# GpSimd instead of VectorE for the differences of weight blocks in the last down projection of a hybrid transformer block

## The chip, the cores and the metric

The kernel runs on one core of a Trainium2 chip. The metric is the device time of one execution in microseconds (us). A core has a matrix engine (TensorE, PE in the profile), three engines for elementwise work (VectorE or DVE, ScalarE or ACT, GpSimd or POOL) and a queue for transfers (SyncE or SP). Each engine works through its own list of instructions in order; semaphores make one engine wait for another. Operands lie in SBUF, and TensorE adds up its products in PSUM.

## The reference

The block has a first feed-forward part, a mixer (differential attention beside a causal convolution) and a second feed-forward part, each scaled by gates that come from a conditioning vector. Sequence length is 256, width 2048, the hidden width of the feed-forward parts 5632, everything float32. The part that the change touches is the last matrix product:

```python
def swiglu(h, w_gu, w_down):
    gu = jnp.einsum('bsd,df->bsf', h, w_gu)
    g, u = jnp.split(gu, 2, axis=-1)
    return jnp.einsum('bsf,fd->bsd', jax.nn.silu(g) * u, w_down)
...
h = modulate(rms_norm(x, ffn2_norm[l]), sh2, sc2)
x = x + FFN_RESIDUAL_WEIGHT * g2[:, None, :] * swiglu(h, ffn2_w_gu[l], ffn2_w_down[l])
```

Here `w_down` is 5632 x 2048, and the product is 256 x 5632 by 5632 x 2048.

## The kernel before

**Split products.** A float32 product is made of three TensorE products of a reduced format. Each operand is split into a high part, which ScalarE casts (`whi`, lines 303 and 510), and a low part, which VectorE subtracts from the original and the high part (`wlo`, lines 305 and 511). The three matmuls of `mm3` (lines 327, 331, 332) are high by high, high by low and low by high; the second reads the weights' low part, and all three have 512 columns.

**The last down projection** is `down_strassen`. It runs in two passes (`np_` 0 and 1), one for each half of the 2048 output columns. A pass has 22 steps, c = 0 to 21. A step loads one tile of weights (`raw`, four blocks of 128x512, 1 MB) and has two blocks of the hidden width, two row tiles and two column blocks.

- A plain step splits its tile in two pairs of blocks (lines 303 and 305, 128x1024 each) and makes eight products, 24 matmuls.
- Steps c = 3, 5, 8, 10, 13, 15 and 17 make seven products instead of eight (Strassen-Winograd), 21 matmuls. They need differences of weight blocks. With b11, b12, b21, b22 for the four blocks, line 545 makes t1 = b12 - b11 and t3 = b22 - b21 in place in one instruction of 128x1024; line 547 makes t2 = b22 - t1 and line 548 t4 = b21 - t2, 128x512 each. The splits follow one another: b11 (128x512), b21 and b22, then t1 and t3, then t4 and t2 (128x1024 each). So line 545 can start once b11's low part is there, the split of t1 and t3 follows line 545, line 547 needs the low parts of b21 and b22, and the split of t4 and t2 follows line 548.
- These steps also need sums of the activations, `sums_of`: a sum of 128x512 (line 483), four of 128x128 (486 to 489), a cast on ScalarE (500) and a low part on VectorE (501). Pass 0 makes all seven sets and six of them are kept for pass 1.

**What sets the order.** A scheduler places the instructions on each engine's list when the program is built, by priorities and its own estimates. High and low parts of weights have four buffers each (`whp`, `wlp`), so a cast waits until TensorE is done with the part four earlier. A plain step takes two buffers of each kind, a seven step all four. Weight tiles have four buffers as well (`rawp`). In a pass, after the last seven step (c = 17), four plain steps follow; VectorE combines the products of the seven steps there (lines 570 to 585). In pass 1 the matmuls of the last two steps are held back and run output tile by output tile, each followed by its scaling, its addition to the residual and its store (lines 528, 529 and 533).

Of the kernel before, what the change touches and what calls it, by code (L numbers as in the profile page):

```python
# [80 lines left out]
def block_kernel(ctx: ExitStack, tc: tile.TileContext, x_in, pos_in, w_ada, small, w_gu1, w_dn1,  # L81
                 w_in, w_out, w_gu2, w_dn2, out):
    nc = tc.nc
# [14 lines left out]
    def nm(s):  # L98
        uid[0] += 1
        return f"{s}_{uid[0]}"  # L100
# [4 lines left out]
    def tmp(shape, dtype=F32):  # L105
        return tmpp.tile(shape, dtype, tag="tmp", name=nm("tmp"))
# [4 lines left out]
    def acc_tile(shape=(P, 512)):  # L111
        return accp.tile(list(shape), F32, tag="acc", name=nm("acc"))
# [350 lines left out]
    def down_strassen(w_dn, aT, a_act, gate_of, evac_last, share, pend, finish):  # L463
# [13 lines left out]
        def sums_of(c):  # L477

            if c in kept:
                return kept[c]  # L480
            a = aT[c]
            full = tmp([P, 2, S])
            nc.vector.tensor_add(out=full, in0=a[:, 0].bitcast(F32), in1=a[:, 1].bitcast(F32))
            a11, a21, a12, a22 = full[:, 0, :P], full[:, 0, P:], full[:, 1, :P], full[:, 1, P:]
            q = tmp([P, 4, P])
            nc.vector.tensor_add(out=q[:, 0], in0=a21, in1=a22)
            nc.vector.tensor_sub(out=q[:, 1], in0=q[:, 0], in1=a11)
            nc.vector.tensor_sub(out=q[:, 2], in0=a11, in1=a21)
            nc.vector.tensor_sub(out=q[:, 3], in0=a12, in1=q[:, 1])
            i = SEVEN.index(c)  # L490
            keep = i < KEPT
            if keep:
                if i < 2:
                    sp = in_c_bc[:, i]
                else:
                    sp = blk([P, 2, 4, P], F32R)
                hi, lo = sp[:, 0], sp[:, 1]
            else:
                hi, lo = tmp([P, 4, P], F32R), tmp([P, 4, P], F32R)
            nc.scalar.copy(out=hi, in_=q)  # L500
            nc.vector.tensor_sub(out=lo, in0=q, in1=hi.bitcast(F32))
            res = [(hi[:, i], lo[:, i]) for i in range(4)]
            if keep:
                kept[c] = res
            return res
# [11 lines left out]
        for np_ in range(2):  # L517
            seven = [None] * 4
            held = []

            def place(i, np_=np_):
                t, n = order[i][0], 2 * np_ + order[i][1]
                return t, n, x[n][:, t, :]

            def final(i, acc, place=place):
                t, n, xs = place(i)
                m = tmp([P, 512])
                nc.vector.tensor_mul(out=m, in0=acc, in1=gbc[n])
                nc.vector.tensor_add(out=xs, in0=xs, in1=m)

            def store(i, place=place):
                t, n, xs = place(i)
                nc.sync.dma_start(out=out[t * P:(t + 1) * P, n * 512:(n + 1) * 512], in_=xs)

            for c in range(NCH):
                share()
                first, last = c == 0, c == NCH - 1
                if c in SEVEN:
                    raw = rawp.tile([P, 4, 512], F32, tag="raw", name=nm("raw"))
                    nc.sync.dma_start(out=raw, in_=w_dn[np_, c].rearrange("p (k n) -> p k n", k=4))  # L540
                    s1, s2, s3, s4 = sums_of(c)
                    (b11,) = split(raw[:, 0:1, :], 1)
                    b21, b22 = split(raw[:, 2:4, :], 2)

                    nc.vector.tensor_sub(out=raw[:, 0:2, :], in0=raw[:, 1:4:2, :], in1=raw[:, 0:2, :])
                    t1, t3 = split(raw[:, 0:2, :], 2)
                    nc.vector.tensor_sub(out=raw[:, 3, :], in0=raw[:, 3, :], in1=raw[:, 0, :])
                    nc.vector.tensor_sub(out=raw[:, 2, :], in0=raw[:, 2, :], in1=raw[:, 3, :])
                    t4, t2 = split(raw[:, 2:4, :], 2)
                    go, end = c == SEVEN[0], c == SEVEN[-1]  # L550
                    if go:
                        if np_ == 0:
                            seven = [acc_tile(), acc_tile(), tp_tile(), tp_tile()]
                        else:
                            seven = [acc_tile() for _ in range(4)]
                    mm3(seven[0], a_act(2 * c, 0), b11, go, end)
                    mm3(plain[0], a_act(2 * c + 1, 0), b21, False, False)
                    mm3(plain[1], s4, b22, False, False)
                    mm3(seven[1], s1, t1, go, end)
                    mm3(seven[3], s3, t3, go, end)  # L560
                    mm3(seven[2], s2, t2, go, end)
                    mm3(plain[2], a_act(2 * c + 1, 1), t4, False, False)
                    tick()
                    if end:

                        p1, p5, p6, p7 = seven
                        u = [tmp([P, 512]) for _ in range(5)]
                        last_pair = np_ == 1
                        nc.scalar.copy(out=u[0], in_=p1)
                        nc.vector.tensor_add(out=u[4], in0=p6, in1=u[0])  # L570

                        def step_1(u=u, p5=p5):
                            nc.vector.tensor_add(out=u[1], in0=p5, in1=u[4])

                        def step_2(u=u, p7=p7):
                            nc.vector.tensor_add(out=u[2], in0=p7, in1=u[4])

                        def step_3(u=u, p5=p5):
                            nc.vector.tensor_add(out=u[3], in0=p5, in1=u[2])

                        def add(i, u=u):

                            t, n, xs = place(i)
                            nc.vector.tensor_mul(out=u[i], in0=u[i], in1=gbc[n])
                            nc.vector.tensor_add(out=xs, in0=xs, in1=u[i])

                        if last_pair:
                            todo += [lambda: (step_1(), add(0), add(1)), lambda: (step_2(), step_3(), add(2)),
                                     lambda: add(3)]
                        else:  # L590
                            todo += [step_1, step_2, step_3]
                    continue
                w = w_tile(w_dn[np_, c])
                if np_ == 1 and c >= NCH - 2:
                    held.append((c, w))
                    if todo:
                        todo.pop(0)()
                    continue
                for k in range(2):
                    for i, (t, n) in enumerate(order):  # L600
                        mm3(plain[i], a_act(2 * c + k, t), w(2 * k + n), first and k == 0, last and k == 1)
                tick()
                if first and np_ == 0:
                    while pend:
                        finish(*pend.pop(0))
                    gbc = gate_of()
                if todo:
                    todo.pop(0)()
            if np_ == 0:
                while todo:  # L610
                    todo.pop(0)()

                def done(i, acc, u, place=place):
                    t, n, xs = place(i)
                    nc.vector.tensor_add(out=u, in0=acc, in1=u)
                    nc.vector.tensor_mul(out=u, in0=u, in1=gbc[n])
                    nc.vector.tensor_add(out=xs, in0=xs, in1=u)
                    nc.sync.dma_start(out=out[t * P:(t + 1) * P, n * 512:(n + 1) * 512], in_=xs)

                todo += [lambda p=plain, u=u: (done(0, p[0], u[0]), done(1, p[1], u[1])),  # L620
                         lambda p=plain, u=u: (done(2, p[2], u[2]), done(3, p[3], u[3]))]
                plain = [acc_tile(), acc_tile(), tp_tile(), tp_tile()]
                continue
            assert not todo
            for i, (t, n) in enumerate(order):
                with tc.issue_after(last_mm[0].ins) if i else nullcontext():
                    for c, w in held:
                        for k in range(2):
                            last_mm[0] = mm3(plain[i], a_act(2 * c + k, t), w(2 * k + n), False,
                                             c == NCH - 1 and k == 1)  # L630
                if i < 3:
                    final(i, plain[i])
                    store(i)
                else:
                    evac_last(2 + n, plain[i], t, gbc[2 + n])
# [820 lines left out]
```

## Time and profile before

| What | Value |
|---|---|
| Time, median of 3 runs | 1838.04 us (1837.12 to 1838.94) |
| The profiled execution: span from first to last instruction | 1835.9 us |
| TensorE, VectorE, ScalarE, GpSimd busy, whole span | 99%, 83%, 52%, 2% |
| Last down projection | about 1598 us to the end |
| Line 545, 14 instructions | 1.22 us each |
| Lines 547 and 548, 14 instructions each | 0.69 us each |

The profiled execution has no time of its own beside its span; the runs' median is 2.1 us more than that span. The page says for each engine how long it was busy. Its timeline gives an instruction's start, its duration, its engine, its line in the kernel, what it writes and reads, and in brackets how long the engine idled before it and what ended that. Instructions of one engine overlap by some hundredths of a microsecond, so the distance from one start to the next is the price of an instruction in an engine that is busy without a gap. A matmul shows 0.39 us, and one starts every 0.227 us.

### The profile page before, as it was taken

To read this page: it belongs to the slowest core of one execution; us is meant where nothing else is said; L and a number is where in the kernel's file an instruction comes from. 1 tells how busy PE (TensorE), PEld (TensorE's weight loads), DVE (VectorE), ACT (ScalarE), POOL (GpSimd) and SP (SyncE) were. 2 spreads that over 40 slices of the span, in tenths; PEclk is the share of its full clock that TensorE was granted. 3 is DMA by queue.
4 is the path that set the end of the run, shared out by engine and by line. 5 is a ranking of instruction groups with operands and counts; after the bars stand their busy time and mean duration, and the time that the engine had idled before them with its cause. 6 is when DMAs were issued, how large, how long until landed. Compare 5 with 4: busy or idle time off the path is not lost.

```text
span 1835.9 us, 22042 instructions
## 1 busy us (share of the span) xinstructions
PE 1812.0 (99%) x8205; PEld 1493.1 (81%) x8205; DVE 1521.8 (83%) x2018; ACT 960.7 (52%) x1477; POOL 28.3 (2%) x29
## 2 busy tenths in 40 slices
PE   7999999999999999999999999999999999999998
PEld 5788888888888887888888788888888888888887
DVE  7889869999888787898999768878877755699877
ACT  6554344444444343566798646664444444455453
POOL 0000000000000000000110000000000000000000
PEclk9999999999999999999999999999999999999999
DMA  9988978889899888765544467899777755555552
GB/s 375 352 307 300 352 272 301 343 306 340 336 322 357 353 343 329 289 256 187 181 159 161 161 229 294 315 335 339 263 273 284 285 197 188 184 206 208 205 210 111
DMA packets 72731, 495.93 MB, mean 270 GB/s; under 512 B 8192, under 2 KB 8624, under 8 KB 15152
## 3 DMA queue, kind: packets, MB, share of 16 engines
q1 hardware_dynamic: 72624, 494.53, 72.2%
q8 instruction: 64, 1.05, 0.2%
q14 instruction: 43, 0.35, 0.1%
HBM read 492.37 MB, written 2.12 MB: 269 GB/s over the span
## 4 chain that ended last, share of the span: by engine, by line
PE 90%; DVE 5%; ACT 2%; issue 1%; DMA 1%; POOL 0%; SPq 0%; POOLq 0%; DVEq 0%; ACTq 0%
PE acc L331 28%; PE acc L332 28%; PE acc L327 28%; DVE wlo L305 2%; PE tp L836 1%; PE tp L332 1%; PE tp L331 1%; PE tp L327 1%; DMA blk<-in_w_gu_dram 1%; PE acc L1123 1%; DVE blk L1015 1%; ACT whi L303 0%; PE tp L392 0%; DMA blk<-in_w_ada_dram 0%; DVE wlo L511 0%
## 5 line engine op out<-in xcount | busy, mean ns | idle before, releaser
L303 ACT CAST whi<-raw 128x1024 fp32r<-128x1024 f32 (+1 forms) x581 | 599.8, 1045 | 610.8 <-PE acc L332 450.3
L331 PE MATMUL acc<-wlo,blk 128*128 128x512 f32 x2340 | 913.5, 390 | 5.8 <-DVE wlo L305 5.8
L327 PE MATMUL acc<-whi,blk 128*128 128x512 f32 x2343 | 913.3, 393 | 1.7 <-ACT blk L401 1.3
L332 PE MATMUL acc<-whi,blk 128*128 128x512 f32 x2340 | 912.5, 390 | 0.1
L305 DVE TENSOR_TENSOR wlo<-raw,whi 128x1024 fp32r<-128x1024 f32 (+1 forms) x581 | 692.6, 1210 | 210.3 <-ACT whi L303 208.8
L331 PEld LDWEIGHTS acc<-wlo,blk 128*128 128x128 f32 x2340 | 439.6, 188 | 99.4 <-DVE wlo L305 10.3
L327 PEld LDWEIGHTS acc<-whi,blk 128*128 128x128 f32 x2343 | 440.0, 188 | 92.8 <-ACT blk L401 1.7
L332 PEld LDWEIGHTS acc<-whi,blk 128*128 128x128 f32 x2340 | 439.3, 188 | 92.4 <-DVE blk L403 0.7
L191 DVE CUSTOM_DVE_ANT_0 raw<-raw,c_bc 128x2048 f32<-128x2048 f32 x142 | 324.1, 2284 | 9.0 <-DMA raw<-in_w_ada_dram 8.8
L510 ACT CAST whi<-raw 128x1024 fp32r<-128x1024 f32 (+1 forms) x56 | 53.0, 946 | 70.2 <-PE tp L332 31.9
L511 DVE TENSOR_TENSOR wlo<-raw,whi 128x1024 fp32r<-128x1024 f32 (+1 forms) x56 | 60.9, 1088 | 19.0 <-ACT whi L510 18.7
L664 ACT COPY blk<-acc 128x512 f32<-128x512 f32 x72 | 41.9, 589 | 60.6 <-PE acc L332 57.9
L1015 DVE SCALAR_TENSOR_TENSOR blk<-blk,cst,blk 128x245 f32<-128x245 f32 (+21 forms) x176 | 70.5, 456 | 0.6 <-ACT blk L1013 0.5
L828 DVE TENSOR_TENSOR blk<-acc,blk 128x512 f32<-128x512 f32 x88 | 56.8, 682 | 0.2
L327 PE MATMUL acc<-blk,blk 128*128 128x512 f32 x104 | 41.3, 400 | 1.0 <-ACT blk L319 1.0
L332 PE MATMUL acc<-blk,blk 128*128 128x512 f32 x100 | 39.0, 392 | 0.0
L331 PE MATMUL acc<-blk,blk 128*128 128x512 f32 x100 | 39.0, 390 | 0.0
L830 DVE TENSOR_TENSOR blk<-blk 128x256 f32<-128x256 f32 x88 | 33.3, 417 | 0.7 <-ACT blk L829 0.7
L829 ACT ACTIVATE blk<-blk 128x256 f32<-128x256 f32 x88 | 32.2, 411 | 2.1 <-DVE blk L828 2.1
L349 DVE TENSOR_TENSOR blk<-tp,blk 128x512 fp32r<-128x512 f32 x44 | 29.9, 684 | 1.6 <-ACT blk L348 1.6
L305 DVE TENSOR_TENSOR blk<-raw,blk 128x1024 fp32r<-128x1024 f32 x24 | 28.8, 1218 | 0.8 <-ACT blk L303 0.8
L450 ACT ACTIVATE tmp<-tp,ada,scales 128x128 f32<-128x128 f32 x36 | 14.8, 459 | 28.0 <-DVE scales L233 15.5
(223 smaller groups left out, 1023.5 us busy)
## 6 DMA issues: line engine op xcount, KB each, us to landing
raw<-in_w_gu_dram SPq DMA_DIRECT2D x161, 1024.0 KB, 5.3
raw<-in_w_ada_dram SPq DMA_DIRECT2D x142, 1024.0 KB, 6.3
raw<-in_w_dn_dram SPq DMA_DIRECT2D x88, 1024.0 KB, 5.2
raw<-in_w_in_dram SPq DMA_DIRECT2D x40, 1024.0 KB, 4.8
raw<-in_w_out_dram SPq DMA_DIRECT2D x16, 1024.0 KB, 4.8
raw<-in_w_gu_dram SPq DMA_DIRECT2D x8, 768.0 KB, 6.0
blk<-in_w_gu_dram SPq DMA_DIRECT2D x10, 512.0 KB, 14.5
blk<-gate_line SPq DMA_DIRECT2D x6, 512.0 KB, 4.9
```

The source lines that it names most:

```text
L191: nc.vector.tensor_tensor_reduce(out=raw, in0=raw, in1=c_bc, scale=1.0, scalar=0.0, op0=ALU.mult, op1=ALU.add, accum_out=ada_cols[g][:, j ...
L303: nc.scalar.copy(out=hi[:, :m, :], in_=rw)
L305: nc.vector.tensor_sub(out=lo[:, :m, :], in0=rw, in1=hi[:, :m, :].bitcast(F32))
L327: nc.tensor.matmul(acc, ah, wh, start=start, stop=False)
L331: nc.tensor.matmul(acc, ah, wl, start=False, stop=False)
L332: return nc.tensor.matmul(acc, al, wh, start=False, stop=stop)
L510: nc.scalar.copy(out=hi[:, :n, :], in_=src)
L511: nc.vector.tensor_sub(out=lo[:, :n, :], in0=src, in1=hi[:, :n, :].bitcast(F32))
L664: last_part[0] = nc.scalar.copy(out=parts[c][:, t, :], in_=accs[t])
L828: nc.vector.tensor_add(out=p[:, t, :], in0=accs[t], in1=p[:, t, :])
L830: nc.vector.tensor_mul(out=p[:, t, 256:], in0=p[:, t, :256], in1=p[:, t, 256:])
L1015: nc.vector.scalar_tensor_tensor(out=y[:, d:], in0=u, scalar=w, in1=y[:, d:], op0=ALU.mult, op1=ALU.add)
```

## The change

In the steps with seven products the three subtractions of weight blocks are issued to GpSimd. Their operands, their sizes and what depends on them stay. All 14 such steps of the two passes are concerned, 42 instructions.

```diff
@@ -542,10 +542,10 @@
                     (b11,) = split(raw[:, 0:1, :], 1)
                     b21, b22 = split(raw[:, 2:4, :], 2)
 
-                    nc.vector.tensor_sub(out=raw[:, 0:2, :], in0=raw[:, 1:4:2, :], in1=raw[:, 0:2, :])
+                    nc.gpsimd.tensor_sub(out=raw[:, 0:2, :], in0=raw[:, 1:4:2, :], in1=raw[:, 0:2, :])
                     t1, t3 = split(raw[:, 0:2, :], 2)
-                    nc.vector.tensor_sub(out=raw[:, 3, :], in0=raw[:, 3, :], in1=raw[:, 0, :])
-                    nc.vector.tensor_sub(out=raw[:, 2, :], in0=raw[:, 2, :], in1=raw[:, 3, :])
+                    nc.gpsimd.tensor_sub(out=raw[:, 3, :], in0=raw[:, 3, :], in1=raw[:, 0, :])
+                    nc.gpsimd.tensor_sub(out=raw[:, 2, :], in0=raw[:, 2, :], in1=raw[:, 3, :])
                     t4, t2 = split(raw[:, 2:4, :], 2)
                     go, end = c == SEVEN[0], c == SEVEN[-1]
                     if go:
```

On VectorE the order changes in pass 0, since the scheduler places anew. This is step c = 5 (`raw_13078`); `in_c_bc` and `tmp` are the sums of activations, of this step and of the next seven steps.

```order
 L511 TENSOR_TENSOR wlo_13090<-raw_13078,whi_13089 128x512
-L489 TENSOR_TENSOR tmp_13082<-tmp_13080,tmp_13082 128x128
+L483 TENSOR_TENSOR tmp_13199<-blk_11373 128x512
 L511 TENSOR_TENSOR wlo_13094<-raw_13078,whi_13093 128x1024
 L501 TENSOR_TENSOR in_c_bc<-tmp_13082,in_c_bc 128x512
-L545 TENSOR_TENSOR raw_13078<-raw_13078 128x1024
-L483 TENSOR_TENSOR tmp_13199<-blk_11373 128x512
-L547 TENSOR_TENSOR raw_13078<-raw_13078 128x512
-L511 TENSOR_TENSOR wlo_13099<-raw_13078,whi_13098 128x1024
-L548 TENSOR_TENSOR raw_13078<-raw_13078 128x512
 L486 TENSOR_TENSOR tmp_13201<-tmp_13199 128x128
 L488 TENSOR_TENSOR tmp_13201<-tmp_13199 128x128
```

The three subtractions are gone, the sums for c = 8 move ahead of them, and the low part of t1 and t3 (`wlo_13099`) comes behind more of the sums. By the low parts of step c = 9 (`wlo_13253` and `wlo_13257`) the seventh set of sums is through:

```order
 L511 TENSOR_TENSOR wlo_13225<-raw_13197,whi_13224 128x1024
 L305 TENSOR_TENSOR wlo_13253<-raw_13249,whi_13251 128x1024
+L501 TENSOR_TENSOR tmp_13585<-tmp_13579,tmp_13584 128x512
 L305 TENSOR_TENSOR wlo_13257<-raw_13249,whi_13255 128x1024
 L511 TENSOR_TENSOR wlo_13296<-raw_13283,whi_13295 128x512
-L487 TENSOR_TENSOR tmp_13407<-tmp_13407,tmp_13405 128x128
-L545 TENSOR_TENSOR raw_13283<-raw_13283 128x1024
```

The sets for c = 13, 15 and 17 were made behind this place before. In pass 1 VectorE's order loses the three instructions and is otherwise the same. GpSimd's list had ended before the projection; now it has three subtractions for each step. These are the steps c = 5 and c = 8 of pass 0, with what each instruction waits for (DMAHW is a load, Pool is GpSimd itself):

```order
L545 TENSOR_TENSOR raw_13078<-raw_13078 128x1024 [waits DMAHW1_49,DMAHW5_49,DMAHW0_49,DVE_49]
L547 TENSOR_TENSOR raw_13078<-raw_13078 128x512 [waits DVE_49,Pool_49]
L548 TENSOR_TENSOR raw_13078<-raw_13078 128x512 [waits Pool_49]
L545 TENSOR_TENSOR raw_13197<-raw_13197 128x1024 [waits DMAHW3_49,DMAHW4_49,DMAHW2_49,DMAHW6_49,DMAHW0_49,DVE_49]
L547 TENSOR_TENSOR raw_13197<-raw_13197 128x512 [waits DVE_49,Pool_49]
L548 TENSOR_TENSOR raw_13197<-raw_13197 128x512 [waits Pool_49]
```

The first and the second subtraction wait for VectorE, and the second and the third for the one before. The order of transfers is unchanged; TensorE's changes in a few rows at c = 3 and c = 5 of pass 0.

## The prediction

> **What bounds the kernel now.** I read the page first, then the busy times of two stretches of the last down projection, then the timelines of VectorE and TensorE inside them, and last every place where GpSimd has worked beside VectorE.
>
> ```profile
> span 1835.9 us, 22042 instructions
> PE 1812.0 (99%) x8205; PEld 1493.1 (81%) x8205; DVE 1521.8 (83%) x2018; ACT 960.7 (52%) x1477; POOL 28.3 (2%) x29
> ```
>
> The profiled execution spans 1835.9 us. The median of the three runs is 1838.04, which is 2.1 us more; I add that at the end. TensorE is busy for 99% of the span, and GpSimd is nearly empty.
>
> ```profile
> core 0: us, PE busy (x) PEld busy (x) DVE busy (x) ACT busy (x) POOL busy (x), PEclk, DMA share, GB/s
> 1607.45:1647.03 39.58, 39.30 (x174) 31.65 (x173) 38.28 (x57) 21.99 (x26) 0.00 (x0) 1.00 0.51 192
> 1785.43:1822.50 37.07, 36.28 (x159) 29.39 (x157) 34.42 (x39) 19.10 (x20) 0.00 (x0) 1.00 0.38 142
> ...
> PE acc L331 <- DVE wlo L305: 0.8, 2, 0.7
> PE acc L327 <- ACT whi L303: 0.2, 1, 0.2
> ```
>
> These rows are two stretches and all that TensorE itself is seen to wait for from 1600 us to the end. The first stretch runs from the first VectorE instruction of step c=3 (pass 0) to the last one of c=9; VectorE is busy 38.28 of 39.58 us. The second is c=15, 16, 17 and the tail of pass 1: 34.42 of 37.07. So VectorE is almost full at both places, and yet TensorE waits for only 1.0 us in the whole projection. **VectorE made cheaper can therefore win about 1 us, and VectorE made dearer costs soon.**
>
> ```profile
> 1620.26 0.39 PE L327 MATMUL acc<-whi,blk 128*128 128x512 f32 x1
> 1625.70 0.39 PE L327 MATMUL acc<-whi,blk 128*128 128x512 f32 x1
> 1649.91 0.39 PE L331 MATMUL acc<-wlo,blk 128*128 128x512 f32 x1
> 1620.74 0.28 DVE L486 TENSOR_TENSOR tmp<-tmp 128x128 f32<-128x128 f32 x1
> 1620.94 0.28 DVE L488 TENSOR_TENSOR tmp<-tmp 128x128 f32<-128x128 f32 x1
> 1621.34 0.68 DVE L511 TENSOR_TENSOR wlo<-raw,whi 128x512 fp32r<-128x512 f32 x1
> 1623.89 1.22 DVE L545 TENSOR_TENSOR raw<-raw 128x1024 f32<-128x1024 f32 x1
> 1625.02 0.68 DVE L483 TENSOR_TENSOR tmp<-blk 128x512 f32<-128x512 f32 x1
> 1625.62 0.68 DVE L547 TENSOR_TENSOR raw<-raw 128x512 f32<-128x512 f32 x1
> 1627.44 0.69 DVE L548 TENSOR_TENSOR raw<-raw 128x512 f32<-128x512 f32 x1
> 1629.31 1.23 DVE L511 TENSOR_TENSOR wlo<-raw,whi 128x1024 fp32r<-128x1024 f32 x1
> 1644.68 2.35 DVE L305 TENSOR_TENSOR wlo<-raw,whi 128x1024 fp32r<-128x1024 f32 x2
> ```
>
> Step 5 on VectorE (c=4's matmuls run meanwhile), from first to last low part. Consecutive starts give the real price of an instruction: 1024 columns 1.13 us (1623.89 to 1625.02), 512 columns 0.60 (1625.02 to 1625.62), 128 columns 0.20. One plain step on TensorE is 24 matmuls from 1620.26 to 1625.70, so 5.44 us and 0.227 a matmul; a step with seven products is 21 matmuls, 4.76 us.
>
> **What is removed.** A seven step loses one 1024-column and two 512-column subtractions on VectorE: 1.13 + 0.60 + 0.60 = 2.33 us, 14 times 32.6 us. All of it lies beside TensorE's work, so none of it is a gain by itself.
>
> **What is moved without being in the diff.** The scheduler pulls the sums of the activations forward. Now all seven sets of pass 0 come ahead of the last low part of c=9; before, the fifth set was only begun there (0.80 us of it done). A set is two 512s and four 128s, 2.0 us, so 1.2 + 2 × 2.0 = 5.2 us come into the first stretch. In it VectorE has 38.28 − 3 × 2.33 + 5.2 = 36.5 us of work, little less than before.
>
> **What is added: the price on GpSimd.** No two-input instruction of that size runs on GpSimd in this trace. Nearest are fills:
>
> ```profile
> 881.77 0.95 POOL L1064 MEMSET blk<- 64x1024 f32 x1
> 882.78 0.95 POOL L1065 MEMSET blk<- 64x1024 f32 x1
> ```
>
> Writing 1024 columns once takes 0.95 us. A subtraction passes two inputs and one output. If the write overlaps the reads, two passes make 1.9 us; if nothing overlaps, three make 2.85. I take the middle, 2.35, and half of it for 512 columns: 4.7 us a seven step, bounds 3.8 and 5.7. Inside the step this is a chain: the first subtraction waits for the low part of b11, the second for the first and for the low parts of b21 and b22, the third for the second. ScalarE's cast of t1 and t3 waits for the first and its cast of t4 and t2 for the third; VectorE's low parts of these queue behind, in order, with the next step's behind them.
>
> The Trainium skill (GPSIMD Engine Reference, 3.1) gives 4497 ns for a two-input addition of 2048 columns; as an estimate that is 2.25 and 1.12 us, 4.5 a step, and the sum below would come out about 1.5 us smaller.
>
> **What decides: may the two engines work at once?** The small powers on GpSimd show it.
>
> ```profile
> 20.23 0.56 POOL L152 TENSOR_TENSOR rstd<-rstd,half 128x1 f32<-128x1 f32 x1 [8.82 <-DVE rstd L151]
> 9.77 1.23 DVE L248 CUSTOM_DVE_ANT_0 blk<-blk,c_bc 128x1024 f32<-128x1024 f32 x1
> 9.96 1.45 POOL L152 TENSOR_TENSOR rstd<-rstd,half 128x1 f32<-128x1 f32 x1 [9.13 <-DVE rstd L151]
> 1042.11 0.70 POOL L1243 TENSOR_TENSOR rv<-rv,half 128x2 f32<-128x2 f32 x1 [22.36 <-DVE rv L1242]
> ...
> 998.19 1.21 DVE L305 TENSOR_TENSOR wlo<-raw,whi 128x1024 fp32r<-128x1024 f32 x1
> 999.33 1.97 DVE L1015 SCALAR_TENSOR_TENSOR blk<-blk,cst,blk 128x240 f32<-128x240 f32 x5
> 998.36 1.92 POOL L152 TENSOR_TENSOR rs<-rs,half 128x4 f32<-128x4 f32 x1 [37.51 <-DVE rs L151]
> 1006.17 1.95 DVE L1015 SCALAR_TENSOR_TENSOR blk<-blk,cst,blk 128x236 f32<-128x236 f32 x5
> 1006.35 1.15 POOL L152 TENSOR_TENSOR rs<-rs,half 128x4 f32<-128x4 f32 x1 [6.07 <-DVE rs L151]
> ```
>
> One column takes 0.56 us, two take 0.70, so four need about 0.98 undisturbed. At 998.36 the same four took 1.92: VectorE was in a subtraction with two SBUF inputs until the next one started at 999.33, 0.97 us later, and 0.97 + 0.95 is what was measured. At 1006.35 VectorE's instructions are 0.39 us short; the one under way ended 0.21 us later, and 1.15 came out. At 9.96 one column took 1.45 instead of 0.56, with the VectorE product (two SBUF inputs) ending 0.9 us later. So GpSimd's reads wait until a two-input VectorE instruction ends, and get in at the next boundary. The reverse, VectorE waiting while GpSimd reads, no row shows: five VectorE instructions after 999.33 took 1.97 against 1.95, but GpSimd then reads four columns only. I take it that the hold works both ways.
>
> The Trainium skill (SBUF — State Buffer, "Who interferes with whom") says just this: a VectorE instruction with two SBUF inputs contends with a GpSimd instruction that reads SBUF, and whoever comes first holds the pair of ports through its whole instruction. The trace agrees for one direction, by the 0.97 us above.
>
> **The sum.** Nearly all VectorE work here has two SBUF inputs, so its time and GpSimd's add up.
> - First stretch: 36.5 + 3 × 4.7 = 50.6 us instead of 39.58, so the last low part of c=9 ends 11.0 us later than now (1644.68 + 2.35 = 1647.03). TensorE first reads it at 1649.91, 2.9 us behind. Loss 11.0 − 2.9 = **8.1 us**.
> - c=10 follows one plain step later and starts with no lead: low parts of a step 0.60 + 3 × 1.13 = 4.0, with GpSimd 8.7, with one plain step (2.26) 11.0 us, against 10.2 on TensorE, and the last cast (1.05) lies bare: **2**.
> - A seven step behind two plain steps has 13.2 us of work against 15.65: nothing. Behind one plain step it lacks 0.8, and once the lead is used up the whole: in pass 0 c=15 0.8 and c=17 2 (four plain steps then pay back), in pass 1 c=5 and c=10 0.8 each: **4.4**.
> - The tail of pass 1:
>
> ```profile
> 1787.71 0.68 DVE L511 TENSOR_TENSOR wlo<-raw,whi 128x512 fp32r<-128x512 f32 x1
> 1797.91 0.68 DVE L511 TENSOR_TENSOR wlo<-raw,whi 128x512 fp32r<-128x512 f32 x1
> 1804.69 1.23 DVE L511 TENSOR_TENSOR wlo<-raw,whi 128x1024 fp32r<-128x1024 f32 x1 [1.12 <-ACT whi L510]
> 1806.12 2.36 DVE L305 TENSOR_TENSOR wlo<-raw,whi 128x1024 fp32r<-128x1024 f32 x2 [0.20 <-ACT whi L303]
> 1820.15 2.35 DVE L305 TENSOR_TENSOR wlo<-raw,whi 128x1024 fp32r<-128x1024 f32 x2
> 1821.42 0.50 PE L331 MATMUL acc<-wlo,blk 128*128 128x512 f32 x1 [0.67 <-DVE wlo L305]
> ```
>
> c=15 starts at 1787.71 and c=17 10.20 us later. From 1806.12 to 1822.5 VectorE has no gap, and TensorE waits for its last low parts (0.67 us). So what c=15 and c=17 fall behind reaches the end. Each adds 4.7 − 2.33 = 2.4 us. VectorE idles 1.12 us ahead of a step's last low part (1804.69) and 0.20 ahead of 1806.12, and can give that once: 4.8 − 1.3, or 3.5; with the bare cast **3.5 to 4**.
>
> Together 8.1 + 2 + 4.4 + 3.7 = 18.2. These ends don't all fall badly at once (a stall early gives VectorE a lead later), so I take 16: 1838.04 + 16 = **1854 us**. With 3.8 a step the stretch loses 2.7 less, the 0.8s vanish, and the tail gives 2: about 10, 1848. With 5.7 it loses 3 more, each close step about 1.8 and the tail 6: about 28, 1866.
>
> Nothing is lost in loads: the weight buffer of a seven step is freed by the same last low part, and four such buffers stand in the queue; the DMA share is 0.51 and 0.38 in the two stretches. If that cover went, a load would be late by at most what VectorE is late, which is counted.
>
> **Rivals.**
> - *VectorE is not held by GpSimd.* Then the work of the first stretch is 36.5 us in 39.58, GpSimd's chain is 4.7 plus up to three waits of about 0.6, 6.5 us, and fits between two seven steps (10.2). For it: the 1.97 against 1.95. Against it: a hold that GpSimd respects and VectorE doesn't. The waits of 1.0 us shrink: 1837.5, not slower. It decides as soon as a 1024-column low part still takes 1.2 us beside GpSimd. Chance 0.17.
> - *Only pass 0 pays.* Without sums pass 1 has 8.7 + 2.26 against 10.2, so near that idle times may swallow it; the first stretch stays: 1838 + 8 = 1846. Chance 0.2.
> - *The chain is the bound, not the shares.* The waits for casts and for each boundary come on top in every close step, some 2 us in each of eight: 1838 + 28 = 1866 or more. Chance 0.08.
> - *Faster by what VectorE saves.* TensorE's 1.0 us of waits is the cap: 1837. It is no different in size from no change.
>
> **How the numbers follow.** The forecast has 0.55, with its own range 1848 to 1864. 0.2% of the time is 3.7 us, about what a measurement can tell from no change. Slower: 0.55 + 0.2 + 0.08 = 0.83, less 0.01 for a small loss in the second rival: 0.82. Same: the first rival and that, 0.16. Faster: 0.02, since no wait of 3.7 us exists. For 8 in 10 the range goes from 1839, which leaves out the first rival, to 1865.
>
> **What would show it.** GpSimd near 4.7 us a seven step, or longer where it waits; low parts (L511, L305) beside it stretched to 2 us and more; TensorE waiting for L511 at c=5 and c=8 of pass 0 for some 8 us together, and for L305 near the end for about 4. If the low parts keep their 1.2 us, the hold is one-sided and the forecast falls; if GpSimd takes under 3 us a step, its price was wrong; if pass 1 shows no waits, the second rival holds.

## The result

The changed kernel takes 1863.57 us (median of 4 runs, 1861.43 to 1865.38) against 1838.49 (4 runs, 1837.12 to 1839.46) for the kernel before on the same chip: ratio 1.014, 95% interval 1.0126 to 1.0154. It is 25.1 us slower. 1854 was forecast, with 1839 to 1865 as the range.

The page of the changed kernel, with the groups of instructions that answer to the change:

```profile
span 1863.6 us, 22080 instructions
PE 1823.6 (98%) x8205; PEld 1495.9 (80%) x8205; DVE 1505.3 (81%) x1976; ACT 958.7 (51%) x1477; POOL 116.3 (6%) x71
...
L511 DVE TENSOR_TENSOR wlo<-raw,whi 128x1024 fp32r<-128x1024 f32 (+1 forms) x56 | 74.0, 1326 | 62.3 <-ACT whi L510 62.2
L510 ACT CAST whi<-raw 128x1024 fp32r<-128x1024 f32 (+1 forms) x56 | 52.9, 944 | 100.2 <-POOL raw L548 32.0
L545 POOL TENSOR_TENSOR raw<-raw 128x1024 f32<-128x1024 f32 x14 | 40.3, 2879 | 616.5 <-DVE wlo L511 616.5
```

GpSimd has 88 us more work, VectorE only 16.5 us less although it lost 42 instructions. Its low parts in the seven steps (L511) take 1326 ns on average; in the kernel before they took 1088:

```profile
L511 DVE TENSOR_TENSOR wlo<-raw,whi 128x1024 fp32r<-128x1024 f32 (+1 forms) x56 | 60.9, 1088 | 19.0 <-ACT whi L510 18.7
```

VectorE also idles 62.2 us ahead of them instead of 18.7: it waits for ScalarE's casts, and 54.6 of the 100.2 us that these casts wait are for GpSimd (32.0 for line 548, 22.6 for line 545). What reaches TensorE, as its largest waits from 1600 us to the end (two more make 0.6 us):

```profile
PE acc L331 <- DVE wlo L511: 4.4, 6, 0.8
PE tp L327 <- ACT whi L510: 3.5, 2, 2.9
PE tp L331 <- DVE wlo L511: 2.8, 4, 0.8
PE acc L327 <- ACT whi L510: 2.3, 3, 0.9
PE acc L331 <- DVE wlo L305: 1.6, 2, 1.5
```

Before there were 1.0 us of them. These rows count from the modelled end of a matmul, so they are too small. I therefore add up, over all starts of matmuls from 1595 us on, by how much a distance exceeds 0.227 us, where it exceeds 0.33: 2.3 us before and 27.3 after, 25.0 more, which is the whole slowdown. (The two spans differ by 27.7 us. The first low part of c=3 in pass 0 already stands 2.2 us later, at 1609.63 instead of 1607.45, where both programs are still the same. That is the difference between two executions.)

How the two engines hold each other is seen in single rows, GpSimd and VectorE at two places of pass 0:

```profile
1625.09 5.73 POOL L545 TENSOR_TENSOR raw<-raw 128x1024 f32<-128x1024 f32 x1 [7.99 <-DVE wlo L511]
1625.54 1.21 DVE L511 TENSOR_TENSOR wlo<-raw,whi 128x1024 fp32r<-128x1024 f32 x1
1626.67 0.68 DVE L501 TENSOR_TENSOR in_c_bc<-tmp,in_c_bc 128x512 fp32r<-128x512 f32 x1
...
1627.88 0.68 DVE L483 TENSOR_TENSOR tmp<-blk 128x512 f32<-128x512 f32 x1
...
1661.92 2.37 POOL L545 TENSOR_TENSOR raw<-raw 128x1024 f32<-128x1024 f32 x1 [5.88 <-DVE wlo L511]
1662.04 3.33 DVE L511 TENSOR_TENSOR wlo<-raw,whi 128x1024 fp32r<-128x1024 f32 x1 [0.20 <-ACT whi L510]
```

At 1661.92 GpSimd came first and took 2.37 us, its undisturbed time. The low part that VectorE began at 1662.04 ended at 1665.37, which is 1.08 us after GpSimd's end: it was held to the end and then ran its usual time. At 1625.09 VectorE was at work without a gap until 1628.5, and GpSimd ended 2.3 us after that. So it was shut out for 3.4 us, over a whole row of VectorE instructions (three sums of 128 columns stand where the dots are).

A second thing shows in the clock, in two stretches of pass 0 beside one of the same length in full clock (columns as in the prediction's table of stretches):

```profile
1633.50:1640.30 6.80, 6.18 (x14) 4.14 (x14) 6.80 (x10) 5.25 (x6) 0.88 (x1) 0.50 0.34 113
1657.40:1664.20 6.80, 6.15 (x15) 4.57 (x15) 6.60 (x6) 3.69 (x5) 2.28 (x1) 0.50 0.66 234
1690.00:1696.80 6.80, 6.80 (x32) 5.63 (x31) 3.77 (x2) 1.49 (x2) 5.03 (x3) 1.00 0.40 167
```

The granted clock is 0.50 for 6.8 us, twice, and TensorE gets through 14 or 15 matmuls instead of 32. The second spell follows TensorE's longest wait, at c=8:

```profile
1653.85 0.40 PE L332 MATMUL tp<-whi,blk 128*128 128x512 f32 x1
1657.16 0.61 PE L327 MATMUL tp<-whi,blk 128*128 128x512 f32 x1 [2.92 <-ACT whi L510]
1658.42 0.80 PE L331 MATMUL tp<-wlo,blk 128*128 128x512 f32 x1 [0.65 <-DVE wlo L511]
1659.44 0.63 PE L327 MATMUL acc<-whi,blk 128*128 128x512 f32 x1
1659.87 0.63 PE L331 MATMUL acc<-wlo,blk 128*128 128x512 f32 x1
```

From 1659.44 on matmuls start 0.43 us apart instead of 0.227. The 14 and 15 of the two spells cost 0.20 us more each, 2.8 and 3.0 us, **5.8 us** together. That leaves 19.2 us of waiting. (The expectation for pass 0 below has 6.4 us for the two spells, from 16 matmuls in each; the rows show 14 and 15.) All this is the profiled execution. The mean granted clock of the four executions is 0.993 to 0.997, so the number of spells need not be the same in each.

### The profile page after: what moved, and what is told of

Its sections match the earlier page's. It is cut to its first block, busy times and chain, and to the rows that moved or that the text cites. A ratio compares the mean times of both kernels' runs of the same rounds, so it can differ in the third digit from the quotient of the medians.

```text
span 1863.6 us, 22080 instructions
## 1 busy us (share of the span) xinstructions
PE 1823.6 (98%) x8205; PEld 1495.9 (80%) x8205; DVE 1505.3 (81%) x1976; ACT 958.7 (51%) x1477; POOL 116.3 (6%) x71
## 4 chain that ended last, share of the span: by engine, by line
PE 83%; DVE 8%; ACT 3%; POOL 2%; DMA 2%; issue 1%; POOLq 0%; SPq 0%; DVEq 0%; ACTq 0%
PE acc L331 26%; PE acc L332 26%; PE acc L327 26%; DVE wlo L305 2%; DVE wlo L511 1%; PE tp L836 1%; POOL raw L547 1%; POOL raw L545 1%; ACT whi L510 1%; DVE raw L191 1%; POOL raw L548 1%; DMA blk<-in_w_gu_dram 1%; PE acc L1123 1%; PE tp L331 1%; PE tp L332 1%
## 5 line engine op out<-in xcount | busy, mean ns | idle before, releaser
L305 DVE TENSOR_TENSOR wlo<-raw,whi 128x1024 fp32r<-128x1024 f32 (+1 forms) x581 | 692.0, 1210 | 206.9 <-ACT whi L303 205.5
L511 DVE TENSOR_TENSOR wlo<-raw,whi 128x1024 fp32r<-128x1024 f32 (+1 forms) x56 | 74.0, 1326 | 62.3 <-ACT whi L510 62.2
L510 ACT CAST whi<-raw 128x1024 fp32r<-128x1024 f32 (+1 forms) x56 | 52.9, 944 | 100.2 <-POOL raw L548 32.0
L545 POOL TENSOR_TENSOR raw<-raw 128x1024 f32<-128x1024 f32 x14 | 40.3, 2879 | 616.5 <-DVE wlo L511 616.5
L152 POOL TENSOR_TENSOR rstd<-rstd,half 128x1 f32<-128x1 f32 x6 | 4.2, 705 | 827.7 <-DVE rstd L151 827.7
L152 POOL TENSOR_TENSOR rs<-rs,half 128x8 f32<-128x8 f32 (+1 forms) x12 | 19.2, 1604 | 231.3 <-DVE rs L151 231.3
```

What stands on the lines that cost most here:

```text
L305: nc.vector.tensor_sub(out=lo[:, :m, :], in0=rw, in1=hi[:, :m, :].bitcast(F32))
L510: nc.scalar.copy(out=hi[:, :n, :], in_=src)
L511: nc.vector.tensor_sub(out=lo[:, :n, :], in0=src, in1=hi[:, :n, :].bitcast(F32))
L545: nc.gpsimd.tensor_sub(out=raw[:, 0:2, :], in0=raw[:, 1:4:2, :], in1=raw[:, 0:2, :])
```

## The experiments

Differences are in medians, against the kernel before on the same chip. All kernels start from the changed one unless the text says otherwise.

**One pass at a time.**

```diff
-                    nc.gpsimd.tensor_sub(out=raw[:, 0:2, :], in0=raw[:, 1:4:2, :], in1=raw[:, 0:2, :])
+                    (nc.gpsimd if np_ == 1 else nc.vector).tensor_sub(out=raw[:, 0:2, :], in0=raw[:, 1:4:2, :], in1=raw[:, 0:2, :])
...
```

The other two differences are edited alike; the second kernel has `np_ == 0`.

> GpSimd makes the differences in pass 1 alone, VectorE in pass 0. Theory (each seven step that follows a single plain step loses its lead, and what the tail falls behind reaches the end): TensorE's extra waits in pass 1 of the changed kernel add up to 8.4 us (9.8 less the 1.4 before), so +8.4 us, 1847, with the granted clock full to the end. Rival (the loss is one of pass 0, where the sums are, and pass 1 only inherits a delay): below +3 us.

> GpSimd makes the differences in pass 0 alone. Theory: +16.5 us, 1855, of which 6.4 us are two spells of halved TensorE clock; together with the run for pass 1 the 25.1 us of the change. Rival (the two passes share one lead, so that either alone costs nearly the whole): +20 us or more.

Measured: pass 1 alone 1848.01 against 1837.68 us, ratio 1.0054 (1.0039 to 1.0069), +10.3 us, more than the 8.4 expected; in the profiled execution its clock is full until the end. Pass 0 alone 1854.10, ratio 1.0087 (1.0072 to 1.0102), +16.4 us, with one spell of half clock of 6.8 us in the profiled execution and not two. Together 26.7 us. The passes don't share a lead; each pays for itself.

**The same chain without reads.** Each subtraction is replaced by fills of the same block, so the differences are left out:

```diff
-                    nc.gpsimd.tensor_sub(out=raw[:, 0:2, :], in0=raw[:, 1:4:2, :], in1=raw[:, 0:2, :])
+                    nc.gpsimd.memset(raw[:, 0:2, :], 0.0)
+                    nc.gpsimd.memset(raw[:, 0:2, :], 0.0)
+                    nc.gpsimd.memset(raw[:, 0, :], 0.0)
...
```

The 512-column subtractions become two fills of 512 columns and one of 256 each.

> In place of each subtraction GpSimd fills the same block with zeros, so the differences are left out; two and a half fills stand for one subtraction, so that the chain stays about 4.9 us a step, but GpSimd reads nothing. Theory (the hold between two-input reads of both engines costs): VectorE's low parts keep 1.2 us, no GpSimd instruction is stretched, at most +4 us. Rival (the chain is longer by itself, 4.9 us against 2.3, and that alone costs): +20 to +25 us, with the same waits of ScalarE for GpSimd.

Measured: 1837.17 against 1837.68 us, ratio 0.9997 (0.9987 to 1.0006). No loss. Groups of this kernel, and a row that shows ScalarE waiting for GpSimd here too:

```profile
L511 DVE TENSOR_TENSOR wlo<-raw,whi 128x1024 fp32r<-128x1024 f32 (+1 forms) x56 | 61.0, 1089 | 52.7 <-ACT whi L510 52.7
L545 POOL MEMSET raw<- 128x1024 f32 x14 | 13.4, 959 | 617.9 <-DVE wlo L511 580.9 <-DMA out_dram<-xall 37.0
ACT whi L510 <- POOL raw L547: 19.7, 8, 3.0
```

A GpSimd chain of about 4.9 us a step, with the wait for it, is free. VectorE is back at 1089 ns, and its idle time of 52.7 us ahead of the low parts does not reach TensorE. So the longer chain by itself costs nothing.

**The same with a read.** The fills become copies of a block onto itself; the differences stay left out:

```diff
-                    nc.gpsimd.memset(raw[:, 0:2, :], 0.0)
+                    nc.gpsimd.tensor_copy(out=raw[:, 0:2, :], in_=raw[:, 0:2, :])
...
```

> As the run with fills, but each fill is a copy of a block onto itself: the differences are left out again, and the one thing that is added to the fills is that GpSimd reads. Theory (the hold is between reads of both engines): low parts beside a copy are stretched, copies behind busy VectorE are stretched, and the loss comes back, +12 to +25 us. Rival (the fills were free because they are a simpler operation with steady 0.5 and 1.0 us, not because they do not read): within 3 us of the kernel before.

Measured: 1872.05 against 1837.75 us, ratio 1.0188 (1.0172 to 1.0203), +34.3 us, above the range that I expected. The first two copies of a step and their longest case:

```profile
1607.08 1.04 POOL L545 COPY raw<-raw 128x1024 f32<-128x1024 f32 x1 [498.63 <-DVE wlo L511]
1608.18 1.04 POOL L546 COPY raw<-raw 128x1024 f32<-128x1024 f32 x1
1621.87 4.99 POOL L545 COPY raw<-raw 128x1024 f32<-128x1024 f32 x1 [6.76 <-DVE wlo L511]
```

Undisturbed a copy takes 1.04 us, a fill 0.96. One read is all that is added in kind (undisturbed, the nine copies of a step take about 5.6 us from start to start where the fills take about 4.9), and the loss goes from nothing to more than the change's own. Why it is above 25 us was not tried; nine instructions a step instead of three, each of which may have to wait, would be a reason.

**The place of the sums.**

```diff
-            nc.vector.tensor_sub(out=lo[:, :n, :], in0=src, in1=hi[:, :n, :].bitcast(F32))
+            last_lo[0] = nc.vector.tensor_sub(out=lo[:, :n, :], in0=src, in1=hi[:, :n, :].bitcast(F32))
...
-                    s1, s2, s3, s4 = sums_of(c)
+                    with tc.issue_after(last_lo[0].ins) if last_lo[0] else nullcontext():
+                        s1, s2, s3, s4 = sums_of(c)
```

> As the changed kernel, but the sums of a step's activations may not be placed on VectorE ahead of the last low part of the seven step before. Theory (5.2 us of sums that were pulled forward stand in front of low parts and keep GpSimd out): TensorE's waits at c=5 and c=8 of pass 0 shrink, no half clock at c=8, +14 to +19 us instead of +25. Rival (the sums' place does not matter): +24 to +26 us.

Measured: 1864.30 against 1837.68 us, ratio 1.0143 (1.0128 to 1.0158), +26.6 us. My expectation fell, but the run does not show that the place of the sums costs nothing. The loss moved: TensorE now waits at c=10, 13, 15 and 17 of pass 0, and no longer at c=8. Of its 15.6 us of waits 9.6 are for the late sums themselves (lines 501 and 502 of this kernel: their cast and low part), where the changed kernel has 0.6. So the edit takes one wait away and adds another. The clock is halved three times, for 3.3, 3.3 and 6.7 us:

```profile
1630.40:1633.70 3.30, 3.30 (x9) 2.59 (x8) 3.30 (x3) 2.66 (x3) 0.00 (x0) 0.50 0.33 72
1691.80:1695.10 3.30, 3.30 (x10) 2.56 (x9) 3.23 (x3) 2.54 (x4) 0.00 (x0) 0.50 0.27 50
1828.40:1835.10 6.70, 6.03 (x14) 4.77 (x15) 5.56 (x6) 4.55 (x6) 0.07 (x1) 0.50 0.43 159
```

**A buffer of their own for the differences.**

```diff
+                    dif = rawp.tile([P, 4, 512], F32, tag="raw", name=nm("raw"))
+                    nc.gpsimd.tensor_sub(out=dif[:, 0:2, :], in0=raw[:, 1:4:2, :], in1=raw[:, 0:2, :])
+                    nc.gpsimd.tensor_sub(out=dif[:, 3, :], in0=raw[:, 3, :], in1=dif[:, 0, :])
+                    nc.gpsimd.tensor_sub(out=dif[:, 2, :], in0=raw[:, 2, :], in1=dif[:, 3, :])
                     (b11,) = split(raw[:, 0:1, :], 1)
...
-                    t1, t3 = split(raw[:, 0:2, :], 2)
+                    t1, t3 = split(dif[:, 0:2, :], 2)
...
```

The three subtractions at their old places are gone, and t4 and t2 are split from `dif`. The second kernel does the same on VectorE.

> GpSimd makes the differences into a weight buffer of their own, so that they wait for the load alone and not for the low parts of b11, b21 and b22. Theory (what costs is that a late and stretched chain stands between two low parts of one step; the hold by itself only moves VectorE's time): the chain runs ahead of the low parts, the loss falls to +2 to +10 us. Rival (VectorE's time under the hold is the bound, so early or late is the same): +20 us or more.

> The same with a buffer of their own, but on VectorE. It shows what the buffer costs: both theories expect within 3 us of the kernel before, if four weight buffers suffice for loads and differences.

Measured: on GpSimd 1855.16 against 1837.50 us, ratio 1.0094 (1.0079 to 1.0110), +17.7 us; on VectorE 1836.67, ratio 0.9994 (0.9985 to 1.0004). The buffer costs nothing, and the chain with a buffer of its own saves about 30% of the loss, between what the two theories expected. It was not early everywhere: five of the 14 first differences still began behind a low part of VectorE and not behind their load, the one of 13.89 us below among them. GpSimd and VectorE in this kernel, pass 0 and then pass 1:

```profile
1630.77 13.89 POOL L543 TENSOR_TENSOR raw<-raw 128x1024 f32<-128x1024 f32 x1 [14.82 <-DVE wlo L511]
1630.61 3.49 DVE L305 TENSOR_TENSOR wlo<-raw,whi 128x1024 fp32r<-128x1024 f32 x3
1642.13 0.28 DVE L487 TENSOR_TENSOR tmp<-tmp,tmp 128x128 f32<-128x128 f32 x1
...
1797.60 3.28 DVE L511 TENSOR_TENSOR wlo<-raw,whi 128x1024 fp32r<-128x1024 f32 x1 [1.50 <-ACT whi L510]
1800.81 4.54 DVE L305 TENSOR_TENSOR wlo<-raw,whi 128x1024 fp32r<-128x1024 f32 x2
```

An instruction of 2.4 us lasted 13.89 us on GpSimd, because VectorE worked without a gap from 1630.61 to 1642.4. In pass 1 it is the other way round: GpSimd is early and free to start, and VectorE's low parts take 3.28 us and twice 2.27. At these two places, either VectorE stretches the chain or the chain stretches VectorE's low parts; to start earlier chooses which.

**Which steps pay.** GpSimd in pass 1 at c=5, 10, 15 and 17 only, the steps behind a single plain step (the close steps below), and then in the steps behind two or more only:

```diff
+                    (nc.gpsimd if np_ == 1 and c in (5, 10, 15, 17) else nc.vector).tensor_sub(out=raw[:, 0:2, :], in0=raw[:, 1:4:2, :], in1=raw[:, 0:2, :])
...
+                    (nc.gpsimd if (np_, c) in ((0, 13), (1, 3), (1, 8), (1, 13)) else nc.vector).tensor_sub(out=raw[:, 0:2, :], in0=raw[:, 1:4:2, :], in1=raw[:, 0:2, :])
```

> GpSimd only in pass 1 at c=5, 10, 15 and 17, the steps that follow a single plain step. Theory (lead): these four carry nearly all of pass 1's loss: in the changed kernel TensorE waits 2.0, 1.4, 1.4 and 2.0 us there and 0.7 more than before at the end, so +7 to +8 us. Rival (every seven step costs the same): four sevenths of pass 1's 8.4, +4.8 us.

> GpSimd only at c=13 of pass 0 and c=3, 8 and 13 of pass 1, the steps that follow two plain steps or more. Theory (lead): no more than +0.8 us, the wait seen at c=3 of pass 1. Rival (every seven step costs the same, 25.1 us through 14): 4 x 1.8 = +7 us.

Measured: the close steps 1846.10 against 1837.50 us, ratio 1.0045 (1.0030 to 1.0060), +8.6 us, a little above the +7 to +8 expected. The others 1840.77, ratio 1.0017 (1.0008 to 1.0027), +3.3 us. Four close steps carry most of pass 1's 10.3 us. Of the others, c=8 and c=13 of pass 1 cost nothing in the trace, and c=3 of pass 1 costs 0.8 us as expected. The rest is c=13 of pass 0, which I had expected to be free: two waits of 1.0 us, and half clock behind them. The profiled execution is the slowest of the ten (1843.29 us, the others 1839.67 to 1841.6), so half clock need not follow in the other nine:

```profile
1675.80:1679.10 3.30, 3.30 (x9) 2.60 (x8) 3.27 (x5) 1.08 (x2) 0.00 (x0) 0.50 0.89 353
```

In this kernel VectorE still makes sums at c=13. In the changed kernel, where they are through by then, c=13 of pass 0 costs nothing. So two plain steps ahead were a lead only where VectorE had no sums to make.

**One kind of difference at a time.** GpSimd makes line 545 only, or lines 547 and 548 only; the rest is on VectorE.

```diff
-                    nc.gpsimd.tensor_sub(out=raw[:, 3, :], in0=raw[:, 3, :], in1=raw[:, 0, :])
-                    nc.gpsimd.tensor_sub(out=raw[:, 2, :], in0=raw[:, 2, :], in1=raw[:, 3, :])
+                    nc.vector.tensor_sub(out=raw[:, 3, :], in0=raw[:, 3, :], in1=raw[:, 0, :])
+                    nc.vector.tensor_sub(out=raw[:, 2, :], in0=raw[:, 2, :], in1=raw[:, 3, :])
```

This is the first kernel; the second has `nc.vector` at line 545 and `nc.gpsimd` at the other two.

> GpSimd makes the 1024-column difference only, VectorE the two of 512 columns. Theory (hold): the instruction takes 2.4 us of the port against 1.13 that it saves, 1.3 us a step against 2.6 for all three; with one entry of GpSimd a step instead of three, +6 to +13 us. Rival (entries and casts behind them are what counts, and the last two differences stand last in the chain): +3 us at most.

> GpSimd makes the two 512-column differences only. Theory (hold): 2.6 us of the port against 1.2 that they save, 1.4 us a step, +6 to +13 us, and the two runs together about the 25 us of the change. Rival (the last two stand behind the first, which is slow; alone they are soon enough): +3 us at most.

Measured: line 545 alone 1843.77 against 1837.75 us, ratio 1.0036 (1.0023 to 1.0049), +6.0 us. Lines 547 and 548 alone 1850.22, ratio 1.0066 (1.0050 to 1.0083), +12.5 us, with two spells of half clock inside the projection. Both are in the ranges, but together 18.5 and not 25. They take nearly the same time on GpSimd (2.4 and 2.6 us), and the pair that stands last in the chain costs twice as much. Part of that is the clock: in the profiled executions half clock takes about 4.4 us of the second kernel and nothing of the first. By the starts of matmuls the waiting is 6.3 us for line 545 and about 10.4 us for the pair. So the time held is not the only measure. That the pair costs more because the last cast and low part of a step follow it at once, and TensorE is next, is a reading; no run tests it.

No kernel here is faster than the one before; the two best (0.9994 and, without the differences, 0.9997) cannot be told from it.

## Why the prediction was right

**Direction and cause held.** TensorE had only 1.0 us of waits to lose, so cheaper VectorE work could win nothing; the run with fills shows it, where VectorE is rid of all differences and the time stays (0.9997). The decisive step was the one that no row of before showed, that VectorE also waits for GpSimd. It holds: 3.33 us for a low part beside GpSimd's 2.37, and 0 against +34.3 us between fills and copies. The first rival (VectorE isn't held) is refuted by the first of these. What no run separates is how much of the 25.1 us each direction costs. Both are large: VectorE was busy for 16.1 us more than the 1489.2 that are left of its 1521.8 us without the subtractions (32.6), and GpSimd's 42 subtractions took 87.9 us where 14 undisturbed chains of 4.98 us (next paragraph) would take 69.7, so 18.2 more.

**The price on GpSimd** was taken as 2.35 and 1.17 us, 4.7 a step. Undisturbed instances of the two 512-column differences:

```profile
1680.79 1.30 POOL L547 TENSOR_TENSOR raw<-raw 128x512 f32<-128x512 f32 x1 [1.35 <-DVE wlo L511]
1682.16 1.29 POOL L548 TENSOR_TENSOR raw<-raw 128x512 f32<-128x512 f32 x1
```

With 2.39 for the first they make 4.98 us, 6% more. The Trainium skill's 4.5 (GPSIMD Engine Reference, 3.1, an estimate from its figure for 2048 columns) is 10% below the trace.

**The terms of the sum**, forecast against what the starts of TensorE's matmuls lost, half clock left out:

| Place | Forecast | Measured |
|---|---|---|
| c=3 to 9 of pass 0 | 8.1 | 7.4 |
| c=10 of pass 0 | 2 | 0 |
| c=15 and 17 of pass 0 | 2.8 | 3.4 |
| c=3 of pass 1 | 0 | 0.8 |
| c=5 and 10 of pass 1 | 1.6 | 3.4 |
| c=15, 17 and the tail of pass 1 | 3.7 | 4.2 |
| Half clock | not foreseen | 5.8 |
| Sum | 18.2, taken as 16 | 25.0 |

The waiting is 19.2 us against 18.2 worked out, but that agreement is partly luck, as c=10 and the close steps of pass 1 show. In the first stretch the last low part of c=9 came 12.0 us later than before (it ends at 1661.24 instead of 1647.03, less the 2.2 us of the two executions), where 11.0 was forecast. That is luck too, as the stretch's row shows:

```profile
1609.63:1661.24 51.61, 45.12 (x175) 34.38 (x174) 41.47 (x64) 23.56 (x30) 22.83 (x9) 0.90 0.41 153
```

The sum filled the whole stretch with VectorE's own work (36.5 us) and GpSimd's (14.1). Here VectorE is busy for 41.5 us, being held included, and idle for 10.1. So the time was not the sum of the two engines' shares; VectorE waited for a chain that came late.

Lowering 18.2 to 16 because a stall gives a lead later was no step with a number behind it, and it went the wrong way.

**The steps that failed.** First, "GpSimd's reads ... get in at the next boundary". They do behind some VectorE instructions only. At c=5 GpSimd waited for a whole run of VectorE's without a gap, 3.4 us, and in the kernel with a buffer of its own 11.5 us. At c=8 it did get in between two VectorE instructions that follow each other without a gap: it started at 1644.12, took 2.78 us, and a sum of 128 columns that VectorE began at 1644.56 took 2.49 us instead of 0.28. What makes a boundary open was not settled. Being shut out makes the chain late where the sum only added up two engines' times. (The 62.2 us that VectorE idles ahead of L511 are no measure of it: with fills, where nothing is held, it idles 52.7 us there.) Second, the sums pulled forward were a term of 5.2 us in the forecast's first stretch; whether they cost that much stays open, since in the run that puts them back TensorE waits for the sums instead. Third, the term that is missing is the clock: the forecast took a wait of TensorE at its own length.

**The rivals.** That pass 0 alone pays is refuted by +10.3 us for pass 1 alone. That the chain is the bound (1866 or more) comes nearest in size, and the chain is indeed what TensorE waits for last. It is also nearer in the close steps: it had some 2 us for each, the six of them at c=15 and 17 of pass 0 and c=5, 10, 15 and 17 of pass 1 cost 1.4 to 2.0 us each, and the forecast had 0.8 each for c=5 and c=10 of pass 1. But with a chain of the same length and no reads the loss is nothing, so it is the hold that makes the chain late.

## What to carry to other kernels

Where VectorE spends its time on instructions with two SBUF inputs, work with SBUF inputs that is moved to GpSimd is not simply taken off it: here both engines' reads waited for one another, and a GpSimd instruction could wait through a whole run of VectorE's. Ask first whether the moved instruction reads: a chain of fills cost nothing here, and one of copies 34.3 us. When a forecast has waits of TensorE that add up to two microseconds or more within 3.4 us, count a chance of half clock behind them as well.

## What the runs showed of the hardware that was not expected

- GpSimd shut out through a run: 13.89 us for an instruction of 2.4 us. The Trainium skill (SBUF — State Buffer, "Who interferes with whom") says that the one that issues second blocks until the first finishes; the trace agrees for single instructions (3.33 us), and shows in addition that "the first" can be a whole row of VectorE instructions.
- TensorE's clock halves for 3.4 or 6.8 us after short waits: after two of 1.1 us at c=5 of the changed kernel, and after two of 1.0 us at c=13 of pass 0 in the kernel with the distant steps. Two waits of 0.8 and 1.0 us at c=17 of pass 1 did not do it. The Trainium skill (TensorE: Matmul & The Clock Gate, Part 1) names a whole idle window of about 3.4 us; here some 2 us in two pieces were enough, and the measurement decides.
- The traces show what decides. Within each of the 13 traces the granted clock changes only at times that lie whole multiples of 3.413 us apart. Between 1595 us and the last matmul, every window of this raster in which the starts of matmuls lose 2.19 us or more at full clock is followed by half clock (eight cases), and none that loses 1.99 us or less; from 2.0 to 2.1 us both occur. So it matters where the raster falls. With pass 0 alone the same two waits at c=5 (1.11 and 1.12 us) lie on both sides of a window's edge at 1630.29, and the clock stays full; in the changed kernel they share the window from 1630.10 to 1633.51. In the kernel with a buffer of its own three windows in a row lose 1.99, 2.07 and 2.03 us, and the clock stays full too.
- A copy on GpSimd takes 1.04 us for 1024 columns, a fill 0.96, a subtraction 2.39.
